# Input projection by seven block products for pairs of column tiles, in a phase ahead of attention, down and output projections

## The chip, the cores and the metric

The kernel runs on one core of one Trainium2 chip. The metric is device time in microseconds (us). Engines: PE (TensorE matmul; PEld is its weight load), DVE (VectorE), ACT (ScalarE), POOL (GpSimd), SP (SyncE, which issues the DMAs). Each has its own instruction queue and works through it in order; they meet at semaphores.

## The reference

One step of a one-layer encoder on 1024 prompt tokens and 32 sample tokens (1056 rows), width 1024, in fp32:

```python
h = _rmsnorm(x, g_mix)
z = h @ w_in                                   # 1056 x 1024 @ 1024 x 8192
qa, fa, va, ga, xb, gb, qc, gc, za, zb, zc = jnp.split(z, offs, axis=-1)
# A: HGRN2 recurrence, 4 heads x 128 (qa fa va ga, 512 columns each)
pa = (oa * silu(ga)) @ w_a_down                # 512 -> 1024
# B: causal conv + RG-LRU, width 1024 (xb, gb)
pb = (hb * silu(gb)) @ w_b_down                # 1024 -> 1024
# C: 4-head attention to 256 memory tokens (qc, gc, 512 columns each)
pc = (oc * silu(gc)) @ w_c_down                # 512 -> 1024
merged = sigmoid(za) * pa + sigmoid(zb) * pb + sigmoid(zc) * pc
y = x + merged @ w_out                         # then a final RMSNorm
```

Memory keys and values are projected from 256 memory rows; the states of conv, LRU and HGRN2 are outputs too.

## The kernel before

All activations lie transposed: 128 features on the partitions, tokens along the free axis, in three groups of 384, 384 and 288 (GN). Each large product is made of three fp32r matmuls: a value is split into a rounded part hi (ACT copy, L40) and a remainder lo (DVE subtract, L43), and mms (L46) issues hi*hi, hi*lo, lo*hi into one PSUM bank. The normalised h stays in SBUF as hh and hl for the whole kernel.

w_in is read in 64 tiles of 128 columns. A tile costs 8 (blocks of 128 rows) x 3 (products) matmuls in each token group: 24 with 384 columns, 24 with 384 and 24 with 288. wload (L107) loads a tile, wprep (L116) splits it, wtile (L132) issues its three groups through slot (L85). After each group, slot lets generator lists take a step: what the vector engines do with an earlier tile, and small matmuls, are so written into the queues between dense groups. PSUM: 3 dense banks (dbank, L68), 5 auxiliary (abank).

Order: phase 0 (norms of 2 memory and 9 token tiles: n_sq, n_mul, n_tr, n_out; projections of w_mem_k and w_mem_v, psmem). Then for B tiles 0 to 4 xb and gb (branch_b, L458: conv, gates pr/pi by matmul, sigmoid, tanh, exp, sqrt, scan), half of w_b_down, B tiles 5 to 7, then the gate logits za, zb, zc (psz) in turn with the down projections psdn (down, L575), with branch A (branch_a, L685; its chunk recurrence hgrn is advanced twice per token group) and branch C (branch_c, L879; chain and attn) ahead of their own down projections. state_out (L653) transposes the B states on PE (ptst), five steps after the last B tile. Everything that a branch makes stays in SBUF until its down projection reads it. At the end psout: merged by w_out for 9 token tiles, residual, final norm.

So every attention and recurrence step stands beside some input projection or down projection, and the DMAs are weights, inputs and outputs alone.

## Time and profile before

| | |
|---|---|
| median of 3 runs | 1197.78 us (1195.06 to 1199.65) |
| the profiled execution | 1196.16 us, span of its instructions 1194.4 us |
| mean granted TensorE clock | 0.997 |
| PE busy | 1179.8 us (99%), 7566 matmuls |
| DVE, ACT, POOL busy | 539.1, 479.9, 236.0 us (45%, 40%, 20%) |
| HBM | 63.49 MB read, 5.93 MB written |

A matmul's shown duration is its latency; matmuls overlap, so what one costs is the distance from one start to the next. The span is 1.8 us less than the execution's time.

### The profile page before, as it was taken

Reading aid. Unit: us, or ns where it says so; the run is one execution under the profiler, and the core shown is the slowest. Engines: PE = TensorE matmul, PEld = TensorE weight load, DVE = VectorE, ACT = ScalarE, POOL = GpSimd, SP = SyncE. Lnnn points to the kernel's source line nnn. Section 1 sums busy time; section 2 is a strip of 40 time slices with the busy share of each in tenths; the row PEclk is TensorE's granted clock in tenths of the full one; section 3 lists DMA queues with packets and bytes.
Section 4 is the critical chain, followed back from the end, with each engine's and each line's share of the span. In section 5 each row is a group of like instructions: output and inputs, shape, how many; then the busy total and the mean of one; then the engine's idle time right before and its main releaser. Section 6 shows DMA issues by size and latency. Waiting matters only on the chain.

```text
span 1194.4 us, 18697 instructions
## 1 busy us (share of the span) xinstructions
PE 1179.8 (99%) x7566; PEld 1161.6 (97%) x7566; DVE 539.1 (45%) x1052; ACT 479.9 (40%) x1043; POOL 236.0 (20%) x425
## 2 busy tenths in 40 slices
PE   8899999999999999999999999999999999999998
PEld 8899999999999999999999999999999999999996
DVE  5957775257711234454544411123456542236322
ACT  6567667367721114353434321111344452233211
POOL 4322222022202232121212101122000001223101
PEclk9999999999999999999999999999999999999999
DMA  8521101211111121111201111112111121105321
GB/s 274 169 63 39 40 21 45 80 38 39 37 36 53 44 63 38 36 43 35 57 27 55 38 32 35 52 44 58 44 46 44 41 54 44 54 27 176 106 93 40
DMA packets 113562, 70.63 MB, mean 59 GB/s; under 512 B 5560, under 2 KB 109668, under 8 KB 113476
## 3 DMA queue, kind: packets, MB, share of 16 engines
q1 hardware_dynamic: 113476, 69.44, 19.4%
q8 instruction: 59, 0.97, 0.4%
q14 instruction: 27, 0.22, 0.1%
HBM read 63.49 MB, written 5.93 MB: 58 GB/s over the span
## 4 chain that ended last, share of the span: by engine, by line
PE 92%; DVE 4%; DMA 2%; issue 1%; ACT 1%; SPq 0%; POOL 0%; POOLq 0%; DVEq 0%; ACTq 0%
PE psz L60 23%; PE psdn L60 14%; PE psgb L60 8%; PE psxb L60 7%; PE psout L60 7%; PE psfa L60 4%; PE psva L60 4%; PE psga L60 4%; PE psqa L60 4%; PE psqc L60 4%; PE psgc L60 3%; PE pr L60 1%; PE pi L60 1%; PE poc L60 1%; DVE ht L241 1%; PE pssa L60 1%
## 5 line engine op out<-in xcount | busy, mean ns | idle before, releaser
L43 DVE TENSOR_TENSOR wlo<-wraw,whi 128x1024 fp32r<-128x1024 f32 (+1 forms) x100 | 107.5, 1075 | 262.7 <-ACT whi L40 261.7
L60 PE MATMUL psz<-hh,whi 128*128 128x384 f32 (+1 forms) x576 | 185.9, 323 | 0.0
L60 PE MATMUL psz<-hh,wlo 128*128 128x384 f32 (+1 forms) x576 | 185.2, 321 | 0.0
L60 PE MATMUL psz<-hl,whi 128*128 128x384 f32 (+1 forms) x576 | 185.0, 321 | 0.0
L40 ACT ACTIVATE whi<-wraw 128x1024 fp32r<-128x1024 f32 (+1 forms) x104 | 96.3, 926 | 79.4 <-PE psdn L60 73.4
L60 PE MATMUL psdn<-ph,whi 128*128 128x384 f32 (+1 forms) x384 | 123.4, 321 | 0.0
L60 PE MATMUL psdn<-ph,wlo 128*128 128x384 f32 (+1 forms) x384 | 123.3, 321 | 0.0
L60 PE MATMUL psdn<-pl,whi 128*128 128x384 f32 (+1 forms) x384 | 123.2, 321 | 0.0
L60 PEld LDWEIGHTS psz<-hh,whi 128*128 128x128 f32 x576 | 108.1, 188 | 0.7 <-issue 0.6
L60 PEld LDWEIGHTS psz<-hh,wlo 128*128 128x128 f32 x576 | 108.2, 188 | 0.3 <-DVE wlo L43 0.3
L60 PEld LDWEIGHTS psz<-hl,whi 128*128 128x128 f32 x576 | 108.1, 188 | 0.0
L584 ACT ACTIVATE sz<-psz 128x384 f32<-128x384 f32 (+1 forms) x72 | 33.3, 463 | 181.7 <-PE psz L60 181.7
L60 PEld LDWEIGHTS psdn<-ph,whi 128*128 128x128 f32 x384 | 72.2, 188 | 0.0
L60 PEld LDWEIGHTS psdn<-pl,whi 128*128 128x128 f32 x384 | 72.1, 188 | 0.0
L60 PEld LDWEIGHTS psdn<-ph,wlo 128*128 128x128 f32 x384 | 72.1, 188 | 0.0
L60 PE MATMUL psout<-hl,mhi 128*128 128x384 f32 (+3 forms) x216 | 68.7, 318 | 0.5 <-DVE hl L43 0.5
L60 PE MATMUL psout<-hh,mlo 128*128 128x384 f32 (+3 forms) x216 | 68.6, 317 | 0.0
L60 PE MATMUL psout<-hh,mhi 128*128 128x384 f32 (+3 forms) x216 | 68.4, 317 | 0.0
L60 PE MATMUL psxb<-hh,wlo 128*128 128x384 f32 (+1 forms) x192 | 62.1, 324 | 0.0
L60 PE MATMUL psxb<-hh,whi 128*128 128x384 f32 (+1 forms) x192 | 61.9, 322 | 0.0
L60 PE MATMUL psxb<-hl,whi 128*128 128x384 f32 (+1 forms) x192 | 61.8, 322 | 0.0
L60 PE MATMUL psgb<-hh,wlo 128*128 128x384 f32 (+1 forms) x192 | 61.7, 321 | 0.0
(297 smaller groups left out, 2905.7 us busy)
## 6 DMA issues: line engine op xcount, KB each, us to landing
wraw<-in_w_in SPq DMA_DIRECT2D x64, 512.0 KB, 4.1
xt<-in_x_prompt SPq DMA_DIRECT2D x8, 512.0 KB, 5.1
wraw<-in_w_b_down SPq DMA_DIRECT2D x16, 256.0 KB, 2.8
wraw<-in_w_out SPq DMA_DIRECT2D x8, 512.0 KB, 4.4
xf<-in_x_prompt SPq DMA_DIRECT2D x8, 512.0 KB
out<-yf SPq DMA_DIRECT2D x8, 512.0 KB, 2.9
wraw<-in_w_mem_k SPq DMA_DIRECT2D x4, 512.0 KB, 3.7
wraw<-in_w_mem_v SPq DMA_DIRECT2D x4, 512.0 KB
```

The costliest lines, as they stand in the source:

```text
L40: nc.scalar.activation(out, in_, AF.Copy)
L43: (eng or nc.vector).tensor_tensor(out, a, hi.bitcast(F32), op=OP.subtract)
L60: nc.tensor.matmul(ps, a, b, start=st, stop=sp)
L241: nc.vector.scalar_tensor_tensor(hts[s][:n], xts[s][:n], rss[s][:n], gts[jobs[s][2]][:n], op0=OP.mult, op1=OP.mult)
L584: nc.scalar.activation(s, R["psz", g], AF.Sigmoid)
```

## The change

The 64 column tiles are taken in 32 pairs (c1, c2). The rows of w_in are halved (512 and 512), the features of h too, and the tokens are halved into two of 528 (HF). So one pair is a 2x2 block product, done by seven block products instead of eight (the Winograd form of Strassen's scheme): p1 = A11 B11, then with S1 to S4 made once from h, and T1, T2, a changed B12 and a changed B21 made per pair on POOL by four 128x512 subtractions. Each of the seven is a slot: 4 blocks x 3 products x 2 quarters of 264 tokens (QF) = 24 matmuls. X, Y, V, Z are PSUM tiles of two banks, two buffers in turn; the sums of products are formed partly in PSUM (slots 2, 5, 6 add to X, V, Z) and partly on DVE (post). Seven forms of h (A11, A12, A22, S1 to S4), each hi and lo, replace hh and hl; S1 to S4 and their splits are made between the norms and the first pairs.

All 32 pairs come first: eight B pairs in turn with z pairs, then per head two A pairs, a z pair and (one head later) a C pair. Their results go to DRAM scratch: sigmoids of z (zd), gc, qc, the B and A products (pbd, pad), memory keys and values. A second phase reads them back: down b with attention advanced beside it, down a, down c, out.

Core of the diff:

```diff
-T_BUFS, T2_BUFS = 45, 24
+T_BUFS, T2_BUFS = 36, 18
+W_RAW, W_HL, P_T, P_ZH = 9, 5, 8, 2
-    dense = ctx.enter_context(tc.tile_pool(name="dense", bufs=3, space=PS))
-    aux = ctx.enter_context(tc.tile_pool(name="aux", bufs=5, space=PS))
+    aux = ctx.enter_context(tc.tile_pool(name="aux", bufs=4, space=PS))
...
+        at(b - 8, loads)
+        at(b - 5, t1)
+        at(b - 4, t2)
+        at(b - 3, lambda: prep(0, "B11"))
+        at(b - 2, lambda: prep(1, "T2"))
+        at(b - 1, lambda: prep(2, "B21"))
+        at(b - 1, t3)
+        at(b, lambda: prep(3, "T1"))
+        at(b + 1, lambda: prep(4, "B12"))
+        at(b + 1, t4)
+        at(b + 2, lambda: prep(5, "B22"))
+        at(b + 3, lambda: prep(6, "B21"))
...
+    ACTS = ("A11", "S2", "A12", "S1", "S3", "S4", "A22")
...
+    def post(k, h):
+        v = lambda t: t[:, :, :QF]
+        if k == 0:
+            cur["p1"] = H("p1")
+            nc.scalar.activation(v2(cur["p1"]), v(cur["X"]), AF.Copy)
+        elif k == 1:
+            cur["u2"] = H("u2")
+            nc.vector.tensor_tensor(v2(cur["u2"]), v(cur["Y"]), v2(cur["p1"]), op=OP.add)
+        elif k == 2:
+            h.c11(v(cur["X"]))
+        elif k == 3:
+            cur["u4"] = H("p1")
+            nc.vector.tensor_tensor(v2(cur["u4"]), v(cur["V"]), v2(cur["u2"]), op=OP.add)
+        elif k == 4:
+            h.c22(v(cur["Z"]), cur["u4"])
+        elif k == 5:
+            h.c12(v(cur["V"]), cur["u2"])
+        else:
+            h.c21(v(cur["Z"]), cur["u2"])
...
+        name, new = (("X", 1), ("Y", 1), ("X", 0), ("V", 1), ("Z", 1), ("V", 0), ("Z", 0))[k]
...
+        for q in range(2):
+            qs = slice(q * QF, (q + 1) * QF)
+            o = ps[:, q, :QF]
+            for i in range(4):
...
+                nc.tensor.matmul(o, wh[:, i, :], fh[:, i, qs], start=st, stop=False, **kw)
+                nc.tensor.matmul(o, wh[:, i, :], fl[:, i, qs], start=False, stop=False, **kw)
+                nc.tensor.matmul(o, wl[:, i, :], fh[:, i, qs], start=False, stop=(i == 3), **kw)
+            advance(fast)
+            if q == 1:
+                advance(chains)
+                run_sched(s)
+        post(k, cur["h"])
...
+            tt(nc.vector, s1, a21, a22, OP.add)
+            tt(nc.vector, s2, s1, a11, OP.subtract)
+            tt(nc.gpsimd, a21, a11, a21, OP.subtract)
+            tt(nc.gpsimd, a12, a12, s2, OP.subtract)
...
+    for s in range(7 * NP):
+        if s == 7 * 16:
+            while chains:
+                advance(chains)
+            bstack.close()
+            a_setup()
+            chains.append(state_out())
+        slot(s)
...
+    slow.append(attention())
+    down("b", pB, 8, {2: lambda: zload("a", 0) if False else None, 6: lambda: late.append(prep_prods(pad, pA))})
+    zload("a", 0)
+    while late:
+        advance(late)
+    down("a", pA, 4, {})
+    while slow:
+        advance(slow)
+    zload("c", 0)
+    late.append(prep_prods(pcd, pC))
+    while late:
+        advance(late)
```

Three places in the queues. First, ACT where the chain of one B tile ends and that of the next begins: before, small steps by token group (whi splits a weight tile; xc and xbp read the conv input out of PSUM; r is the gate).

```order
L40 ACTIVATE whi<-wraw 128x1024
L467 ACTIVATE xc<-psxb,VT 128x384
L468 ACTIVATE xbp<-psxb 128x384
L541 ACT_TABLE_LOAD
L541 ACTIVATE r<-r,sneg 128x384 x2
L541 ACTIVATE r<-r,sneg 128x288
```

And ACT in the change, from the square root of one tile (th) over the first steps of the next (xw, sgb) to the reading of X after slot 0 of the z pair (p, the tile p1 of the code).

```order
L669 ACT_TABLE_LOAD
L669 ACTIVATE th<-th 128x1056
L42 ACTIVATE whi<-wraw 128x512 x2
L42 ACTIVATE whi<-T_1658 128x512
L42 ACTIVATE whi<-wraw 128x512
L626 ACTIVATE xw<-xbp,VT 128x1059
L627 ACT_TABLE_LOAD
L627 ACTIVATE sgb<-gb 128x1056
L42 ACTIVATE whi<-T_1620 128x512
L270 ACTIVATE p_1804<-X 128x528
```

The chain's steps are now whole rows of 1056, and the reading of X stands behind three of them and a table load in ACT's queue.

Second, PE at the attention of the last head: before, its last products (poc) stand between dense groups of psz.

```order
L60 MATMUL psz<-hh_83,wlo 128x384
L60 MATMUL poc<-prh,mh 128x256
L60 MATMUL poc<-prl,mh 128x256
L60 MATMUL poc<-prh,ml 128x256
...
L978 MATMUL poc<-prs,cv 128x32 x2
L60 MATMUL psz<-hh_84,whi 128x384
```

In the change, from the last matmul of down a on (scores pssa and pssb, transposes ptp of the exponentials ex).

```order
L62 MATMUL psdn<-ph,wlo 128x288
L1098 MATMUL ptc<-ident,ck 128x128 x2
L62 MATMUL pssa<-mh,qh 128x256
...
L62 MATMUL pssb<-mh,ql 128x256
L1146 MATMUL ptp<-ident,ex 128x128 x6
L62 MATMUL pssa<-mh,qh 128x256
```

From there all three groups' scores, transposes and products of head 3 follow each other with no psdn between them; the next psdn row is that of down c.

Third, SP where the phases meet, in the change alone (before, only weight and input loads stand here): the last stores of the first phase, then the first loads of the second (sz are sigmoids of z, praw the B products).

```order
L155 DMA gcd_115<-zh 128x528
L155 DMA qcd_119<-zh 128x528 x2
L155 DMA gcd_115<-zh 128x528
L956 DMA wraw<-in_w_b_down 128x8x128
L1001 DMA sz<-zdb_96 128x384 x2
L1001 DMA sz<-zdb_96 128x288
L975 DMA praw<-pbd_120 128x384 x2
L975 DMA praw<-pbd_120 128x288
L956 DMA wraw<-in_w_b_down 128x8x128
```

Every load of the second phase now stands behind the store of the last pair's last quarter.

## Rows read from the trace of the kernel before

**Rows 1.** The page, parts 1 and 4: busy engines; chain that ended last, by engine.

```profile
PE 1179.8 (99%) x7566; PEld 1161.6 (97%) x7566; DVE 539.1 (45%) x1052; ACT 479.9 (40%) x1043; POOL 236.0 (20%) x425
PE 92%; DVE 4%; DMA 2%; issue 1%; ACT 1%; SPq 0%; POOL 0%; POOLq 0%; DVEq 0%; ACTq 0%
```

**Rows 2.** The chain in order of time, merged: start us, us, what.

```profile
76.05 3.19 PE psgb L60 x24
355.10 5.76 PE psdn L60 x36
360.86 11.53 PE psz L60 x72
```

**Rows 3.** Timeline, PE and DVE, end of phase 0: start us, us, what, [idle before].

```profile
43.77 0.28 PE L60 MATMUL psmem<-hh,whi 128*128 128x256 f32 x1
...
45.44 0.28 PE L60 MATMUL psmem<-hh,wlo 128*128 128x256 f32 x1
49.87 0.43 PE L60 MATMUL psxb<-hh,whi 128*128 128x384 f32 x1
55.62 1.09 PE L251 MATMUL pt<-ident,ht 128*128 128x128 f32 x8 [1.33 <-DVE ht L241]
61.81 0.54 DVE L43 TENSOR_TENSOR hl<-pt,hh 128x128 fp32r<-128x128 f32 x2 [1.97 <-ACT hh L40]
```

**Rows 4.** Timeline of POOL and DVE, phase 0: a subtraction on POOL, two norm multiplies.

```profile
28.14 2.41 POOL L43 TENSOR_TENSOR wlo<-wraw,whi 128x1024 fp32r<-128x1024 f32 x1 [0.57 <-ACT whi L40]
28.64 3.00 DVE L241 SCALAR_TENSOR_TENSOR ht<-xt,rsr,gx 128x1024 f32<-128x1024 f32 x1
34.75 1.28 DVE L241 SCALAR_TENSOR_TENSOR ht<-xt,rsr,gx 128x1024 f32<-128x1024 f32 x1
```

**Rows 5.** Groups by line and form, DVE and ACT: xcount | busy us, mean ns | idle.

```profile
L43 DVE TENSOR_TENSOR wlo<-wraw,whi 128x512 fp32r<-128x512 f32 x32 | 22.7, 708 | 73.5 <-ACT whi L40 72.6
L552 DVE TENSOR_TENSOR_SCAN xc<-r,ig 128x384 f32<-128x384 f32 x8 | 7.7, 958 | 0.3
L40 ACT ACTIVATE whi<-wraw 128x1024 fp32r<-128x1024 f32 x72 | 76.2, 1058 | 25.6 <-PE psdn L60 19.7 <-PE psmem L60 4.4 <-DMA wraw<-in_w_mem_k 1.5
L40 ACT ACTIVATE whi<-wraw 128x512 fp32r<-128x512 f32 x32 | 20.1, 628 | 53.8 <-PE psdn L60 53.8
L506 ACT ACT_TABLE_LOAD x8 | 10.3, 1283 | 0.1
L501 ACT ACTIVATE th<-r,spos 128x384 f32<-128x384 f32 x16 | 10.1, 631 | 0.0
```

**Rows 6.** Timeline, one step of the recurrence in branch A.

```profile
502.20 0.39 PE L803 MATMUL pu<-v,kt 128*128 128x128 f32 x2
503.57 0.26 ACT L796 ACTIVATE kt<-pu 128x128 f32<-128x128 f32 x1
```

**Rows 7.** Timeline, one token group of attention, head 0: scores, scaling, split of transposes.

```profile
840.15 0.28 PE L60 MATMUL pssa<-mh,qh 128*128 128x256 f32 x1
844.67 0.35 DVE L955 TENSOR_SCALAR ex<-ex,ri 128x256 f32<-128x256 f32 x1
849.55 0.82 PE L963 MATMUL ptp<-ident,ex 128*128 128x128 f32 x6
850.67 1.02 DVE L43 TENSOR_TENSOR prl<-ptp,prh 128x384 fp32r<-128x384 f32 x2 [3.56 <-ACT prh L40]
```

**Rows 8.** Windows (busy us of each engine, clock, DMA share, GB/s), and DMA issues.

```profile
20.00:30.00 10.00, 9.94 (x87) 9.74 (x85) 7.46 (x9) 8.09 (x16) 7.41 (x6) 1.00 0.92 292
...
wraw<-in_w_b_down SPq DMA_DIRECT2D x16, 256.0 KB, 2.8
```

**Rows 9.** Windows near the start: PE, PEld, DVE, ACT, POOL busy; PEclk.

```profile
8.00:9.00 1.00, 0.00 (x0) 0.00 (x0) 1.00 (x1) 0.00 (x0) 0.03 (x1) 1.00 1.20 367
...
11.00:12.00 1.00, 1.00 (x7) 1.00 (x6) 0.84 (x2) 1.00 (x2) 0.00 (x0) 0.50 1.06 267
...
13.00:14.00 1.00, 1.00 (x10) 1.00 (x10) 0.70 (x1) 0.40 (x1) 0.00 (x0) 0.93 1.12 406
```

More of the change, by code (lines that the diff above doesn't have):

```diff
@@ L377, in feed @@
             yield
-            for s in range(4, 10):
+            for s in range(4, nj + 2):
                 norm_step(s)
+                if s == 8:
+                    forms.append(form_ops())
                 yield
-        start(feed())
+            done[0] = True
+        chains.append(feed())
         for n in range(8):
@@ new lines @@
+            if n == 3:
+                chains.append(vec_consts())
+            chains.append(mem_evac(which, j, ps))
+            advance(chains)
+            advance(forms)
+        while not done[0]:
+            advance(chains)
+            advance(forms)
+        while chains:
+            advance(chains)
+        run_sched(-3)
+        while forms:
+            advance(forms)
+        run_sched(-2)
+        run_sched(-1)
+    fb = p1stack.enter_context(tc.tile_pool(name="forms_b", bufs=1, reuse_waits="tile"))
@@ L653, in state_out @@
     def state_out():
-        for _ in range(5):
-            yield
         pt = abank("ptst")
@@ L865, in branch_a @@
[L865 to L872 removed]
+            nc.vector.tensor_scalar(f[:, :NT], f[:, :NT], oml[:, j:j + 1], lb[:, j:j + 1], op0=OP.mult, op1=OP.add)
+            yield
+            lf, b = T1("lf"), T1("b")
+            nc.scalar.activation(lf[:, :NT], f[:, :NT], AF.Ln)
@@ new lines, in KS, with slot2 @@
+    def KS(name):
+        return (kp.tile([128, NT], F32R, tag="kh", name=name + "h"), kp.tile([128, NT], F32R, tag="kl", name=name + "l"))
+    slow, late = [], []
+    par = [0]
+    def slot2(ms, after=None):
+        issue(ms)
+        par[0] = (par[0] + 1) % 2 if len(ms) == 12 else 0
+        if par[0] == 0:
+            advance(slow)
+        if after is not None:
+            after()
+        advance(late)
+    loaded, prepped, wtiles = {}, {}, []
+    for src, kt in (("w_b_down", 8), ("w_a_down", 4), ("w_c_down", 4)):
+        for it in range(8):
+            wtiles.append((I[src][0], kt, it * 128))
@@ new lines, in branch_c, with attention @@
+        ev_qc(0)
+        yield
+        kvsplit(1, vr)
+        ev_qc(1)
+        for t in range(8):
+            if t in (2, 4, 6):
+                trans(t // 2 - 1)
+            if t in (3, 5, 7):
+                pv(t // 2 - 1)
+            if t in (0, 2, 4):
+                scores(t // 2)
+                scale_(t // 2)
+            if t == 1:
+                ev_qc(2)
+            if t < 7:
+                yield
+    def attention():
+        for j in range(4):
+            yield from branch_c(j)
@@ L1028, in xload, with wgen @@
             nc.sync.dma_start(xf[t][:n], xs[t])
-    down(lambda k: prods_c[k], C_ZC, "last", AH_C, lambda: next_phase("fp", 1))
+    def wgen():
+        for k in range(6):
+            wout_load(k)
+            yield
+            yield
+            wout_prep(k)
+    down("c", pC, 4, {1: lambda: late.append(wgen())})
+    while late:
+        advance(late)
+    for k in range(6, 8):
+        wout_load(k)
+        wout_prep(k)
     gf = wpool.tile([128, D], F32, tag="hi", name="gf")
@@ L1079, in after @@
                 xload(t + 3)
-        slot(ms, after)
+        slot2(ms, after)
         advance(late)
@@ L1089 @@
             out_unit(t, gi)
-    assert not fast and not slow and not tail and not late
-    phase.close()
+    assert not fast and not slow and not late and not chains
 _INS = ['x_prompt', 'x_sample', 'mem_prompt', 'cache_mem_k', 'cache_mem_v', 'state_hgrn', 'state_conv', 'state_lru',
```

1366 lines of the change are left out of this document (706 added, 660 removed).

## Prediction

> **What bounds the kernel now.** I read the page's shares first: PE is busy for 1179.8 us of a span of 1194.4, the other engines for less than half, and the chain that ended last is 92% PE [rows 1]. So the time is PE's own work, and the chain in order of time shows at what pace: 24 matmuls of 288 columns take 3.19 us (132.9 ns each), a column tile of w_in 11.53 us (so 173.8 ns for each of its 48 of 384), a down tile of four blocks 5.76 us, each starting where the last ended [rows 2]. Then the timeline for the one place that is not so dense, the end of phase 0: the first projection matmul starts at 49.87, a wait of 1.33 us for a norm follows, and the last norm tile is written at 62.35 [rows 3]. Whatever shortens PE's work shortens the kernel, as long as PE still has something to do at each moment; that second condition is what the change touches.
>
> **The saving.** 15 matmuls of 256 columns start from 43.77 to 45.44, 119.3 ns apart [rows 3]; between that and 132.9 for 288, a matmul of 264 columns takes 119.3 + (8/32) x 13.6 = 122.7 ns, a slot of 24 takes S = 2.94 us. Before: 64 tiles x 11.53 = 737.9 us. After: 32 pairs x 7 slots x 24 = 5376 matmuls x 122.7 = 659.6. **-78 us**. It is not the eighth of 738 (92), because a matmul costs about 13 ns beyond its columns at 2.4 GHz and there are 768 more. Gates, recurrence, attention, down and out keep their matmuls (the gates' quarters of 264 cost 0.05 us more per tile).
>
> **Phase 0.** Before, the first projection group runs while late norms are made; counting its wait and the transposes in between (3.6 us), projection starts in effect at 53.5. After, S1 to S4 need every token. Up to the last norm the work of PE, DVE and DMA is much the same, so it ends at about 59 (62.35 less the 4 us that it stood behind a projection group). Then, from 0: DVE makes s1 and s2, four half operations of 1056 columns at 1.3 us (1.28 for 1024 [rows 4]); POOL a21 and a12, four at 2.5 us (2.41 for 1024); then DVE owes five forms of two 1.3 us remainders and four weight remainders of 0.7 us [rows 5]: 5.2 + 13 + 2.8 = 21 us on DVE, 10 on POOL. PE can run slots 0 and 1, but slot 2 waits for p1, which stands on ACT behind all five form copies; the fourth of them waits for POOL, so p1 is ready at about 22, and slot 3 waits for u2, behind all remainders on DVE, at about 25. Contiguous work would have been at 8.8 there: 16 us idle at least. One row shows more: beside a POOL subtraction from 28.14 to 30.55 a DVE multiply that takes 1.28 us alone took 3.00 and ended 1.1 us after POOL did [rows 4]. So POOL's work adds to DVE's in part; if all of it did, u2 would be ready at about 32 and PE idle for 23. I take 19, with 5.5 for the later start: **+24** (10 if ACT and DVE interleave well and the norms end sooner, 32 if all adds).
>
> The Trainium skill states this as a rule (SBUF — State Buffer, section Who interferes with whom): DVE operations with two SBUF inputs and POOL operations that read SBUF take an exclusive lock, the loser waits for the whole instruction. The row above agrees. By the rule alone phase 0 would be +29 instead of +24.
>
> **The B pairs.** Each reading of a PSUM tile has one slot of slack before PE needs the tile again: p1 (ACT) before slot 2, u2 before 3, c11 before 4, u4 before 5, c22 before 6, c12 and c21 (DVE) before the next slots 0 and 1. These readings stand in their queues behind the chain of the last B tile, now in whole rows of 1056: on DVE 1.3 us each and 2.8 for the scans (0.958 for 384 [rows 5]), on ACT 1.1 to 1.2 (1.058 for 1024, 0.628 for 512, more with an operand per partition) and 1.28 per table load. Followed from slot 2 of a B pair (time 0; ACT comes to exp 0.5 before it): exp with its table load ends at 2.0, POOL's square at 4.5, DVE's th at 6.6 (one POOL subtraction in its way), sqrt 7.7, weight copy 8.3, remainder 9.0, u4 9.7; slot 5 wanted it at 3S = 8.8: **0.9 late**. Then DVE: ig, remainder, c22, scans, remainder, c12, 6.9 us to 16.6; the next slot 0 wanted it at 5S + 0.9 = 15.6: **1.0 late**. Then the last multiply, remainder and c21 to 19.6, and on ACT xw, table load, sigmoid, copy, p1 to 24.4; slot 2 of the z pair wanted it at 7S + 1.9 = 22.5: **1.9 late**. The rest of the z pair is light and the delay does not build up. 3.8 x 7 tiles (the eighth is the next part): **+28**. Bounds: 8 if only one of the waits binds; 50 if DVE becomes the limit: per two pairs DVE has 14 remainders, 10 readings and 13.6 us of chain, 31 us, POOL 16, together 47 where PE has 44.
>
> **state_out.** Ahead of slot 112 the rest of the eighth chain is written at once, and ptst follows slot 112 on PE; it needs POOL's copy of the scan's end. From the last gate matmul: four sigmoids 2.0, tanh 1.2, table and exp 2.5, square 2.5, th 1.3, sqrt 1.1, ig 1.3, scans 2.8, copies 0.8 = 15.7 us, of which slot 112 covers 2.9. Behind ptst stands all of PE. **+13** (8 to 18). Before, the same transpose was written five steps later, between psz groups.
>
> **A pairs.** The recurrence's kt comes 1.63 us after its pu started [rows 6], the next is due after 12 matmuls (1.47) and a step of about 1 us. Slack 0.85; ACT's copy and reading (1.25 per slot) and DVE's come between, and three times per head PE waits for pot with 4 banks instead of 5. About 2.5 per head: **+10** (3 to 25).
>
> **Where the phases meet.** All loads stand behind the last store on SP, so nothing is fetched until 1.3 us after the last slot. Ahead of the eighth B product lie two weight tiles, two rows of sz, eight of praw, six of attention: 7.8 MB. At 292 GB/s, the best ten-microsecond window, that is 27 us; at 275, 28; a 256 KB load lands 2.8 us after its issue, 1.9 of it not transfer [rows 8]. PE ends the first down tile at about 34, with 11.5 us of work in it: **+23** (14 to 30).
>
> **Down a to down c.** Attention needs 49 steps, down b and a give 37; head 3 from its scores on is left to the drain. One token group takes 4.9 us from its first score matmul to its scaled exponentials, and 2.1 more from transposes to their remainders [rows 7]. With about 3 us of DVE work first, three groups in a row take 24 us, 8 of them PE's own. Then the store of the last product, and loads of sz and four products (2.7 MB, 9.8 us at 275 GB/s, with landing and splits some 15) which all stand behind it; the first tile has 5.8 us of work, so 9 us more of idle. **+25** (15 to 35).
>
> **The rest.** Two of eight w_out tiles are prepared after down c: **+2** (0 to 4). In the trace PE did nothing from 8 to 9; from 11 to 12 the granted clock was 0.50, the level of 1.2 GHz, and late in 13 to 14 it was back at 2.4 [rows 9]. That is some 4 us at half rate, 2 us lost; three long idles at that price: **+6** (0 to 15).
>
> **Sum.** -78 + 24 + 28 + 13 + 10 + 23 + 25 + 2 + 6 = +53. On the profiled execution's 1196.2 us, which lies within the three runs and 1.6 under their median: **1249 us**.
>
> **Rivals.** (1) *DVE and ACT keep up.* They are below half busy now, and each reading has a slot of slack. Then phase 0 falls to 10, the B pairs to 8 at most, A to 3, the clock to 0: 24 + 28 + 10 + 6 becomes 21, about 1202; with the B pairs at 0 and the meeting at its lower end, 1185, faster. It decides where all costs together come under 78; the four gaps that depend on no queue (phase 0, state_out, meeting, drain) are 85 by themselves. Chance 0.17, of it 0.12 faster. (2) *DVE is the limit in the B half.* POOL's and DVE's work add up (47 us for 44): 50 instead of 28, and phase 0 at 32: about 1280. For it the row of 3.00 us [rows 4], against it the light z pairs. 0.20. It is what the lock of the Trainium skill's page SBUF — State Buffer (Who interferes with whom) would do here. (3) *The seven products don't save what they should*, the matmul of 264 columns costing as much as that of 288, 132.9 ns: 714 us, saving 24, about 1303. Against it the 119.3 of 256 columns. 0.04. My forecast, 1215 to 1270: 0.55; the rest lies between.
>
> **Numbers.** 0.5% is 6 us, about what a measurement can tell from no change. Faster 0.13, same 0.06, slower 0.81. The range of 1195 to 1285 leaves about 0.15 below and 0.05 above.
>
> **What would show it.** After: X, Y, V, Z matmuls 122 to 123 ns apart inside a slot; PE busy well under 95%; PE waits by tile: S forms and p1 before the first V, then V for DVE, X for ACT once per B pair, ptst for POOL by about 13 us, psdn of the first tile for praw, pssa/ptp/poc after down a for DVE and ACT. I am wrong if the slots of the B pairs follow each other without waits, if the loads at the meeting are spread over the first phase's end, or if head 3's drain takes under 10 us.

## The result, and the profile after

The changed kernel takes 1292.62 us (median of 4 runs, 1290.78 to 1296.88) where the kernel before takes 1197.38 (4 runs beside it): a ratio of 1.080, 95% interval 1.076 to 1.084. It is slower, by 95 us; 53 were forecast, and the time lies 8 us above the range. The profiled execution is 1294.4 us with a span of 1292.4.

The page first: part 1, and of part 2 the granted clock in 40 equal slices.

```profile
PE 1149.5 (89%) x8382; PEld 1114.1 (86%) x8382; DVE 762.4 (59%) x1152; ACT 529.4 (41%) x1026; POOL 403.0 (31%) x463
PEclk9868999999999997999999999999899999699999
```

PE is busy for 30 us less than in [rows 1], and idle for 143 us where it was idle for 15. The granted clock is below nine tenths in some of the slices. The stretches show where. Columns as in [rows 8]: the stretch, its length, busy time of PE, PE's weight loads, DVE, ACT and POOL, granted clock, DMA share, GB/s.

```profile
0.00:68.36 68.36, 49.78 (x354) 47.12 (x354) 43.70 (x77) 36.18 (x69) 26.25 (x38) 0.89 0.64 195
68.36:98.44 30.08, 9.30 (x50) 8.79 (x49) 26.33 (x21) 12.58 (x15) 24.27 (x7) 0.61 0.18 53
98.44:488.17 389.73, 359.67 (x2833) 353.53 (x2833) 278.57 (x298) 196.00 (x301) 147.75 (x131) 0.98 0.25 76
488.17:898.26 410.09, 384.29 (x3079) 374.94 (x3077) 221.61 (x354) 167.38 (x356) 132.87 (x168) 0.98 0.22 68
898.26:925.88 27.62, 13.38 (x56) 11.70 (x55) 12.73 (x26) 12.18 (x28) 0.00 (x0) 0.75 0.96 305
925.88:1090.70 164.82, 161.72 (x1016) 157.50 (x1014) 90.56 (x217) 49.06 (x124) 29.27 (x50) 0.99 0.40 123
1090.70:1127.74 37.04, 17.84 (x71) 13.14 (x69) 17.01 (x49) 11.72 (x34) 3.75 (x11) 0.64 0.30 94
1127.74:1183.00 55.26, 51.20 (x289) 49.64 (x289) 42.16 (x69) 24.69 (x46) 25.04 (x23) 0.93 0.65 210
```

They are: phase 0 up to the first slot; the first two slots and the wait for the forms; slots 2 to 111 (the B half); slots 112 to 223 (the A half); the meeting; down b and a; the drain; down c. A busy PE can be PE at half clock, so I set each stretch against what its matmuls need at full clock: 121.3 ns for 264 columns (row below), 173 for 384 [rows 2], 132.9 for 288, 119.3 for 256, 108 to 112 for 128. For the B half that is 110 slots of 2.91 and 192 gate matmuls, 343.5 us of 389.7.

| stretch | length | needed | lost | forecast |
|---|---|---|---|---|
| phase 0, to slot 2 | 98.4 | 45.8 | 52.6 (before, up to 60: 13.4) | +24 |
| B half | 389.7 | 343.5 | 46 | +28 |
| A half with ptst | 410.1 | 369.8 | 40 | +23 |
| meeting | 27.6 | 8.6 | 19 | +23 |
| down b and a | 164.8 | 153.7 | 11 | 0 |
| drain | 37.0 | 8.4 | 29 | +25 |
| down c and out | 164.6 | 146.2 | 18 | +2 |

The same count gives 36 us lost in the kernel before (13 of them before 60 us, 7 in the attention stage, 7 after it), so 180 more are lost and PE's work is 82 less: the 98 us between the two spans. The seven products themselves came as forecast. Two matmuls of a slot, first and last of 24 (start, us, engine, line, operation):

```profile
143.07 0.28 PE L302 MATMUL Y<-S2h,whi 128*128 128x264 f32 x1
...
145.86 0.28 PE L304 MATMUL Y<-S2h,wlo 128*128 128x264 f32 x1
```

23 steps in 2.79 us: 121.3 ns, a slot of 2.91 us. 224 slots take 652 us, against 737.9 before: 86 saved, 78 forecast.

What PE waited for, whole span (who <- for whom: us in total, times, longest). In the trace's names p is p1 (line 270) or u4 (line 278), u is u2.

```profile
PE X L302 <- ACT p L270: 23.0, 8, 15.3
PE psdn L62 <- ACT ph L42: 20.4, 4, 8.2
PE V L302 <- DVE p L278: 12.4, 8, 1.8
PE pt L362 <- DVE ht L352: 12.4, 7, 4.1
PE ptst L685 <- POOL ST L678: 12.0, 1, 12.0
PE V L302 <- DVE u L273: 10.4, 12, 1.5
PE ptc L1098 <- DMA ck<-in_cache_mem_k: 9.0, 3, 6.0
PE pot L876 <- DVE on L869: 7.9, 4, 2.0
PE ptp L1146 <- DVE ex L1138: 6.3, 7, 3.4
PE X L304 <- DVE wlo L45: 5.5, 1, 5.5
```

The forecast named most of these. New are the wait of slot 0 for a weight remainder (5.5) and the cached keys (9.0).

### The profile page after: what moved, and what is told of

Its sections match the earlier page's. It is cut to its first block, busy times and chain, and to the rows that moved or that the text cites. A ratio compares the mean times of both kernels' runs of the same rounds, so it can differ in the third digit from the quotient of the medians.

```text
span 1292.4 us, 21318 instructions
## 1 busy us (share of the span) xinstructions
PE 1149.5 (89%) x8382; PEld 1114.1 (86%) x8382; DVE 762.4 (59%) x1152; ACT 529.4 (41%) x1026; POOL 403.0 (31%) x463
## 4 chain that ended last, share of the span: by engine, by line
PE 54%; DVE 17%; ACT 10%; DMA 8%; issue 7%; POOL 3%; SPq 1%; DVEq 0%; POOLq 0%; ACTq 0%
PE psdn L62 10%; PE psout L62 7%; DVE wlo L45 5%; PE V L302 4%; PE V L304 3%; PE V L303 3%; PE Z L302 3%; PE Z L304 3%; PE Z L303 3%; ACT whi L42 2%; PE X L302 2%; PE X L304 2%; PE X L303 2%; POOL hT L498 2%; DMA wraw<-in_w_in 2%
## 5 line engine op out<-in xcount | busy, mean ns | idle before, releaser
L45 DVE TENSOR_TENSOR wlo<-wraw,whi 128x512 fp32r<-128x512 f32 (+1 forms) x193 | 193.5, 1004 | 113.9 <-ACT whi L42 113.8
L42 ACT ACTIVATE whi<-wraw 128x512 fp32r<-128x512 f32 (+1 forms) x200 | 123.9, 639 | 59.2 <-PE Z L303 17.7
L302 PE MATMUL X<-A12h,whi 128*128 128x264 f32 x256 | 75.7, 296 | 23.0 <-ACT p L270 23.0
L302 PE MATMUL V<-S4h,whi 128*128 128x264 f32 x256 | 76.2, 298 | 12.4 <-DVE p L278 12.4
L302 PE MATMUL V<-S1h,whi 128*128 128x264 f32 x256 | 76.4, 298 | 10.4 <-DVE u L273 10.4
L1011 POOL TENSOR_TENSOR sz<-sz 128x384 f32<-128x384 f32 (+1 forms) x48 | 50.9, 1080 | 80.6 <-DVE sz L1010 80.4
L302 PE MATMUL Y<-S2h,whi 128*128 128x264 f32 x256 | 75.0, 293 | 0.4
L302 PE MATMUL X<-A11h,whi 128*128 128x264 f32 x256 | 75.0, 293 | 0.0
L304 PE MATMUL V<-S4h,wlo 128*128 128x264 f32 x256 | 74.9, 292 | 0.0
L303 PE MATMUL V<-S4l,whi 128*128 128x264 f32 x256 | 74.5, 291 | 0.0
L303 PE MATMUL V<-S1l,whi 128*128 128x264 f32 x256 | 74.3, 290 | 0.0
```

Source lines behind the costliest of these rows:

```text
L42: nc.scalar.activation(out, in_, AF.Copy)
L45: (eng or nc.vector).tensor_tensor(out, a, hi.bitcast(F32), op=OP.subtract)
L302: nc.tensor.matmul(o, wh[:, i, :], fh[:, i, qs], start=st, stop=False, **kw)
L303: nc.tensor.matmul(o, wh[:, i, :], fl[:, i, qs], start=False, stop=False, **kw)
L304: nc.tensor.matmul(o, wl[:, i, :], fh[:, i, qs], start=False, stop=(i == 3), **kw)
L1011: nc.gpsimd.tensor_tensor(m, m, z, op=OP.add)
```

## The experiments

My theory after the result: the seven products save what they should; the waits are links of in-order queues (one late operation on ACT or POOL delays a reading that stands behind it), not full engines. The rivals: DVE is the limit wherever PE waits; or the division into two phases costs it all, whatever the products. Ratios are to runs of the kernel before made beside each version, gains in us to the 1292.6 of the changed kernel. Its four runs spread over 6 us (1290.8 to 1296.9): the gains of 5 to 6 us below are just clear of that spread, one of 3 isn't.

**e1: ptst later.**

```
-            chains.append(state_out())
+            chains.append(state_late())   # 14 yields, then state_out
```

> The changed kernel with the transposition of the B states (ptst) written 14 slots later, nothing else. In the changed kernel PE waited 12.0 us for it, and the granted clock was 0.5 for about 14 us around it. If the place of that one instruction is the cause, the 12 us disappear, the clock stays full there, and the time falls by 12 to 18 us, from 1292.6 to 1275 to 1281. The rival: PE waits for the drained eighth chain in any case, at another instruction (the gates or the next reading of a bank); then the wait turns up under another name and the time falls by less than 4 us.

1282.9 us, ratio 1.072 [1.070, 1.074]: 10 less. The wait for ST is gone; in its place PE waits 4.8 us for p1 in slot 114, because ACT still has the drained eighth chain to do first. Partly the rival, then.

**e2: the differences on DVE.**

```
-            tt(nc.gpsimd, a21, a11, a21, OP.subtract)
-            tt(nc.gpsimd, a12, a12, s2, OP.subtract)
+            tt(nc.vector, a21, a11, a21, OP.subtract)
+            tt(nc.vector, a12, a12, s2, OP.subtract)
```

> The changed kernel with the two differences A11-A21 and A12-S2 made on DVE instead of POOL. On POOL they took 21.4 us (four of 5.35) while DVE's remainders beside them were stretched from 1.2 to 2.9 each. If the two engines take turns (the lock), DVE alone needs 69.28 to about 93 for the forms instead of 97.7, PE's slot 2 starts 4 to 6 us earlier, and the time falls by 4 to 6 us, to about 1287. If instead POOL and DVE work side by side and POOL is only slow, 4.8 us more on DVE make it later: the last remainder ends at about 100 and the time rises by 2 us or so.

1287.5, ratio 1.076 [1.074, 1.078]: 5 less, as the lock says. The rows of the changed kernel (POOL, then DVE; x2 are two operations):

```profile
70.59 14.62 POOL L498 TENSOR_TENSOR hT<-hT 128x1056 f32<-128x1056 f32 x2 [13.36 <-DVE s L498]
85.17 6.81 POOL L498 TENSOR_TENSOR hT<-hT,s 128x1056 f32<-128x1056 f32 x2
83.98 5.72 DVE L45 TENSOR_TENSOR S3l<-hT,S3h 128x1056 fp32r<-128x1056 f32 x2 [3.48 <-ACT S3h L42]
89.74 5.60 DVE L45 TENSOR_TENSOR S4l<-hT,S4h 128x1056 fp32r<-128x1056 f32 x2
```

and of e2, all on DVE:

```profile
74.67 2.41 DVE L498 TENSOR_TENSOR hT<-hT 128x1056 f32<-128x1056 f32 x2
85.83 2.41 DVE L45 TENSOR_TENSOR S3l<-hT,S3h 128x1056 fp32r<-128x1056 f32 x2
```

Two operations take 2.41 us on DVE alone; beside POOL the same remainders took 5.72. While DVE had an unbroken row of them (69.28 to 80.4), POOL's first two took 14.62. This agrees with the exclusive lock that the Trainium skill states (SBUF — State Buffer, Who interferes with whom). POOL's first operation was done at about 82.9, where ACT's copy of its result began: 12 us for one operation, behind a whole row of DVE's and not behind a single one.

**e3: own buffers for raw w_out tiles.**

```
-            wraws[k] = wpool.tile([128, D], F32, tag="raw", name="wraw2")
+            wraws[k] = wop.tile([128, D], F32, tag="wo", name="wraw2")   # bufs=2, loaded two ahead
```

> The changed kernel with two buffers of their own for the raw w_out tiles, which are loaded two ahead, instead of the pair that they share with the w_c_down tiles. In the changed kernel the down projection of c took 61 us from its first to its last matmul for 46 us of matmuls, with loads of 3.3 us, a copy and a remainder one after the other on the chain. If the shared buffers are the cause, that stage falls by 8 to 12 us and the time to about 1282. If the cause is DVE (77% busy in that stage, POOL's additions in its way), it falls by less than 4.

1286.5, ratio 1.076 [1.073, 1.078]: 6 less. Down c takes 49.5 us instead of 55.3 (not the 61 of the text), at a DVE of 94%. In the changed kernel each w_out load had stood behind the release of a w_c_down tile. The gain lies between the figures of the two theories: the shared buffers cost some of the stage, and with them gone DVE is close to full.

**e4: order of loads.**

```
     wload(0)
+    raws = [load_prod(src) for src in pbd]
     zload("b", 0)
```

> The changed kernel with the loads at the meeting of the phases in another order: the first weight tile, the eight products, then the gate row, the next weight tile and the loads of attention. In the changed kernel 27 us pass from the last slot to the dense part of the second phase, at 313 GB/s and a DMA share of 0.99. If bandwidth sets it, 0.5 + 4.3 MB ahead of the last product instead of 8.4 MB let PE reach its eighth product at about 16 to 18 us instead of 25: the time falls by 6 to 9 us, to about 1285. If latency or the splitting of products (eight of about 2 us on ACT and DVE, 16 us in all) sets it, it falls by less than 4.

1293.7, ratio 1.081 [1.079, 1.084]: nothing gained. The rows of ACT tell why:

```profile
903.74 5.38 ACT L42 ACTIVATE ph<-praw 128x384 fp32r<-128x384 f32 x12
921.57 0.52 ACT L1092 ACTIVATE tg<-graw 128x384 f32<-128x384 f32 x1 [12.46 <-DMA graw<-gcd]
922.00 2.41 ACT L42 ACTIVATE ph<-praw 128x384 fp32r<-128x384 f32 x6
```

Four products were split by 909; then attention's tanh, whose load now came last, held the queue for 12.5 us with four products behind it. A load moved back is a wait moved forward on the engine that reads it in program order.

**e5: p1 and u2 ahead of the last forms.**

```
     S2, S1 split
+    slot(0)
+    slot(1)
     S3, S4, A22 split
```

> The changed kernel with the first pair's slots 0 and 1 and their readings p1 and u2 written ahead of the copies and remainders of S3, S4 and A22, and with buffers for p1 and u2 that don't lie where hT lay. In the changed kernel p1 stood on ACT behind all five form copies, was made at 97.8, and slots 2 and 3 (whose forms A12 and S1 were ready at 80.5) came after that. If the order on ACT and DVE is the cause, slots 2 and 3 run before 97 and the time falls by 5 to 7 us, to about 1286. If the forms as such set the end of phase 0 (slot 4 needs S3, and the reading of X a buffer that hT held), slot 4 starts where slot 2 started and that is the whole gain, 5.8; a gain under 3 would mean that DVE's extra reading delays the remainders as much as it helps.

1289.5, ratio 1.078 [1.076, 1.079]: 3 less, not clear of noise. The trace shows what moved. Slot 2 now follows slot 1 at 82.8, but slot 3 waits 8.3 us for u2: u2 stands on DVE behind a weight remainder, that on ACT's copy, that on POOL's weight subtraction, and this on POOL behind the two differences, until 91.6. One link of the chain removed, the next one held.

**e6: attention after every group of down a.**

```
-        par[0] = (par[0] + 1) % 2 if len(ms) == 12 else 0
+        par[0] = 0
```

> The changed kernel with one step of attention after every group of the down projection of a instead of after every second one, so that 48 of its 49 steps are written beside down groups and head 3 is not left to a drain. In the changed kernel 38 us pass between the last matmul of down a and the first of down c, of which PE's own work is 9.4 at full clock. If uncovered attention is the cause, what is left is the store of the last product, the loads and the splits, 12 to 15 us, and the time falls by 15 to 23 us, to about 1273. The rival: a step of attention takes longer on DVE and ACT than a group of 12 matmuls of PE (2.1 us), so the same waits move into down a, and the time falls by less than 8.

1278.4, ratio 1.067 [1.065, 1.069]: 14 less. Head 3's scores and products now lie between the groups of down a with waits of 0.5 us in all; left are 4.4 and 2.6 for cached keys and 6.6 for the last product.

**e7: a third pair of banks.**

```
+    banks(n_aux=2, n_dense=3)            # B half; 4 and 2 elsewhere
+        pr, pi = pg[:, :n], pg[:, 256:256 + n]   # both gates in one bank, pieces of 256
```

> The changed kernel with three pairs of PSUM banks for X, Y, V and Z in the B half instead of two (and two single banks for the gates instead of four, with both gates of 256 columns in one bank and a fifth piece of 32 columns). Each reading then has a second slot of slack. In the changed kernel PE waited some 29 us in the B half for p1, u2 and u4, 4.7 us in each of the tiles. If late readings on in-order queues with one slot of slack are the cause and no engine is full, at least two thirds go, and the time falls by 18 to 28 us, to about 1270. If DVE is the limit (POOL's and DVE's work taking turns, 47 us for 44 of PE), the waits stay and only change their names: less than 8.

1291.7, ratio 1.079 [1.076, 1.082]: no gain. Waits of PE in the B half, in the changed kernel (105 to 487 us):

```profile
PE V L302 <- DVE p L278: 12.4, 8, 1.8
PE V L302 <- DVE u L273: 9.5, 8, 1.5
PE X L302 <- ACT p L270: 7.7, 7, 1.5
```

and in e7:

```profile
PE X L310 <- ACT p L278: 12.5, 7, 1.8
PE Z L310 <- DVE gb L618: 10.2, 7, 1.5
PE V L310 <- DVE p L286: 5.0, 7, 0.7
```

29.6 us there, 27.7 here. Waits that stay and change their names are what the text gave for a full DVE, so this run by itself doesn't rule that out; e9 does. The lines have another reason as well: p1, u4 and c22 read a tile that PE goes on adding to two slots later, in the same bank, so a third pair of banks gives these three readings no slack.

**e8: PE kept busy in three waits.** 40 transpositions of the identity ahead of slot 0, 60 ahead of slot 2, 60 ahead of down b.

> The changed kernel with idle transpositions of the identity on PE where it waits anyway: 40 ahead of the first slot, 60 ahead of the first pair's slot 2, 60 ahead of the second phase. They give PE work of about 6.5 us each at full clock and delay nothing that is ready. In the changed kernel the granted clock was 0.5 for 17 us from 63.5, for 17 us from 87.4, and for two stretches of 6.8 from 903 and 917. If the clock falls because PE stands idle, these stretches shrink, slot 2 takes 2.9 us instead of 5.2, and the time falls by 4 to 8 us, to about 1287. If the clock there doesn't matter, because something else sets the pace, nothing changes (within 2 us).

1287.2, ratio 1.076 [1.074, 1.077]: 5 less. Granted clock from 60 to 80 us 0.91 instead of 0.59, from 80 to 104 0.79 instead of 0.64, from 900 to 930 0.89 instead of 0.77.

**e9: two ACT operations of the B chain one slot later.**

```
-        nc.scalar.activation(sg[:, :NT], G[:, :NT], AF.Sigmoid)
         (copies of the states)
         yield
+        nc.scalar.activation(sg[:, :NT], G[:, :NT], AF.Sigmoid)
...
         th = (xc + 1) * th                                     # DVE
+        yield
         nc.scalar.activation(th[:, :NT], th[:, :NT], AF.Sqrt)
```

and one yield less between the last gates' sigmoids and the tanh.

> The changed kernel with two of the B chain's ACT operations written one slot later (the sigmoid of G after xw, the square root after the multiply that it reads), and two light steps made one, so that the chain still has 14. In the changed kernel's B pair the square root waited on ACT for DVE's th; behind it stood a weight copy, behind that on DVE a remainder and u4, which PE's slot 5 waited 1.75 us for; and the sigmoid with its table load stood ahead of p1, which the z pair's slot 2 waited for, and then u2. If such chains of waits across the in-order queues are the cause, the 12.4 us for u4 and most of the 17 for p1 and u2 go, and the time falls by 15 to 25 us, to about 1273. If DVE's own load is (73% busy, with POOL's subtractions stretching its operations), the waits move to c12, c22 or another reading and the time falls by less than 6.

1267.2, ratio 1.058 [1.057, 1.060]: 25 less, the largest single gain. The chain of waits as the changed kernel has it (ACT, then DVE; slot 5 had been due at 154.7):

```profile
152.89 1.09 ACT L669 ACTIVATE th<-th 128x1056 f32<-128x1056 f32 x1 [1.88 <-DVE th L668]
153.89 1.14 ACT L42 ACTIVATE whi<-wraw 128x512 fp32r<-128x512 f32 x2
154.53 1.43 DVE L45 TENSOR_TENSOR wlo<-wraw,whi 128x512 fp32r<-128x512 f32 x1 [1.68 <-ACT whi L42]
155.89 0.69 DVE L278 TENSOR_TENSOR p<-V,u 128x528 f32<-128x528 f32 x1
```

and the B half of e9 (105 to 455 us):

```profile
PE V L302 <- DVE u L273: 11.5, 14, 1.4
PE V L302 <- DVE p L278: 1.2, 1, 1.2
```

DVE and POOL have the same operations as before; only the order changed. So a full DVE isn't what bounded the B half: slots 2 to 111 take 26 us less with the same work. 17 of the 26 are the waits (29.6 to 12.7). The three stretches at half clock inside the B half are gone too, which is 5 us. The moves of e9 were not run one by one.

**e10: eight ordinary products in the same two phases.** No forms of sums, no subtractions of weights, four weight blocks split instead of seven.

```
-    ACTS = ("A11", "S2", "A12", "S1", "S3", "S4", "A22")
+    ACTS = ("A11", "A12", "A11", "A12", "A21", "A22", "A21", "A22")
```

> The two phases of the changed kernel with eight ordinary products of 24 matmuls per pair instead of the seven (A11 B11 + A12 B21 and so on: no forms of sums, no subtractions of weights, four weight blocks split instead of seven, every result read once). PE gets 32 x 24 matmuls of 121 ns more, 93 us. If about half of what the seven products save on PE goes into their own waits (19 to 22 us at the forms, some 25 at the readings in the B half), it takes only 30 to 45 us more than the seven: 1322 to 1338. If all of the loss lies in the division into two phases (the meeting, the drain, the stores and loads), which both have, it takes 85 to 93 us more: 1378 to 1386.

1298.9, ratio 1.085 [1.083, 1.087]: only 6 more than the seven, below both theories' figures. From slot 4 to ptst no wait of PE is listed:

```profile
66.17:93.09 26.92, 26.08 (x193) 25.77 (x193) 11.41 (x18) 10.12 (x13) 1.29 (x2) 0.88 0.38 100
93.09:480.00 386.91, 376.21 (x3098) 376.01 (x3096) 173.57 (x192) 165.58 (x243) 56.76 (x68) 0.99 0.24 72
```

(The last ten of these 387 us are the wait for the drained eighth chain, at ptst.) Of the 93 us that seven products take off PE, 87 went back into what only the seven lose: by the count of the table 23 us ahead of slot 2, 46 in the B half (the eight lose 0.5 there) and 19 in the A half. The eight stand 102 us above the kernel before, with 7 of it in projection matmuls (745 us for 738). The other 95 lie in what both versions share: the two phases with their stores and loads, the chain in whole rows, the order of the steps, the smaller buffers. No run here takes these apart, and none has the seven products without the phases; e18 takes 42 of them back by order and buffers alone.

**e11: e4's order, attention held until the last block of the first down tile, and e6.**

```
-                    if k % 2:
+                    if k == kt - 1 or c != "b" and k % 2:
                         advance(slow)
```

> The changed kernel with the order of loads of the run e4 (products first), attention's first steps held until the last block of the first down tile, and attention advanced after every group as in the run e6. In e4 the gain was lost because attention's tanh, which waits for its loads, stood on ACT ahead of the copies of products 4 to 7 (ACT idle from 909 to 921.6). If bandwidth and this one place set the meeting, the first down tile ends some 8 us earlier than in e6: 1278.4 - 8 = about 1270. If latency or splits set it, it stays at e6's 1278, or rises by what three lost steps of attention cost at the end of down a (up to 8 us).

1281.3, ratio 1.070 [1.068, 1.072], 3 above e6, whose runs overlap with its own. At the meeting it is ahead: 34 us after its last slot it has begun 118 down matmuls, the changed kernel 91. The end of down a takes it back: between down a and down c 20.0 us pass without a down matmul, in e6 9.7, and the three lost steps of attention fall there.

**e12: sums of the first half of the columns before the last norms.**

```
+                if s == 10:
+                    done[1] = True     # columns 0:264 of s1, s2, a21, a12 may be made, on DVE
```

> The changed kernel with the sums S1, S2, A11-A21 and A12-S2 made for the first half of the token columns while the norms of the last tokens still run, all on DVE. In the run with all differences on DVE the forms ended about 5 us earlier than in the changed kernel. Half of the 9.6 us of sums now lies beside the norms, where DVE was some 70% busy. If DVE's work after the last norm sets the end of phase 0, PE's slot 2 starts 4 to 5 us earlier still than in that run, and the time falls to about 1283 (10 under the changed kernel). If the norms are already bound by DVE (PE waited 12.4 us for their multiplies), what is gained behind the last norm is lost ahead of it: about 1287.

1287.4, ratio 1.075 [1.072, 1.077], as e2 within the interval. The agreement with the second figure of the text is luck, for the edit moved nothing. The first of the sums stands behind the last norm copy (71.74 to 72.0), as in e2, where it starts at 70.00:

```profile
72.27 1.24 DVE L497 TENSOR_TENSOR s<-hT 128x1056 f32<-128x1056 f32 x1
```

So this is e2 once more, with the forms' operations in another order, and its question stays open. Slot 0 started at 71.4 (69.1 in e2), but all of that delay was there before any sum: the third norm multiply from the end started at 54.41, in e2 at 52.09.

**e13 and e14: together.** e13 has the edits of e1, e2, e3, e5, e6, e8 and e9; e14 those and the five named in its text.

> The single changes of the runs before in one kernel: the B chain's two ACT operations one slot later, ptst 14 slots later, the differences on DVE, p1 and u2 ahead of the last forms, own buffers for raw w_out tiles, attention after every group of down a, transpositions that keep PE busy in three waits. Their gains by themselves against 1292.6: 25.4, 9.7, 5.1, 3.1, 6.1, 14.2, 5.4, together 69. If they are independent: about 1224. If waits hide behind each other (the ACT queue at ptst and in the B chain, DVE at the end of phase 0), a fifth to a third of it is lost: 1238 to 1248.

> The kernel of the run e13 with five more edits: the forms' first half of columns early; the last head's product split straight from SBUF instead of stored and loaded, and the other three products and the first gate row of c fetched during the last tile of down a (PE waited 6.3 us there for a product); the order of loads of e4 with attention held until the last block of the first down tile, and four extra steps of attention in down b; four buffers instead of two for keys and cached keys (PE waited 9.0 us for cached keys). If each goes for what its wait says (5, 7, 5, 8) this takes another 20 to 25 us: about 1200, as the kernel before. If the waits are taken over by the next one in line (attention's own chain of scores, scaling, transposes), about 1212.

e13: 1234.9, ratio 1.032 [1.030, 1.033], 58 of the 69 us: the causes add up but for a sixth. e14: 1241.3, ratio 1.037 [1.035, 1.039], slower than e13. In both of them stands this (e13, PE; line 289 are the idle transpositions):

```profile
86.48 6.71 PE L289 MATMUL warm<-ident 128*128 128x128 f32 x60
92.95 0.37 PE L309 MATMUL X<-A12h,whi 128*128 128x264 f32 x1
```

With e2 and e5 nothing waits there any more, and the filler itself is the wait. Of what e14 loses against e13, 4 us are there when slot 2 starts (97.0 against 93.0) and 3 come behind the last slot, where PE waited 11.2 us for cached keys instead of 6.5: more buffers for loads that are still issued late don't help. The early sums of e12 are late in e14 too.

**e15 to e17: which of the remaining waits.** e15 is e13 without those 60 transpositions, with these two edits and four buffers instead of two for the keys; e16 and e17 add to e15.

```
+            if t == 3 and j < 3:
+                fetched[j + 1] = fetch(j + 1)            # e15: the next head's loads
+            split(own[0][0][:, cs], own[0][1][:, cs], s)  # e15: head 3, in place of store and load
+                if c == "b" and g == 1 and it % 2 == 0:
+                    advance(slow)                         # e16, with e11's order
+                if k == 0:
+                    post(k, cur["h"])                     # e17: p1 ahead of the chain's step
```

> The kernel of the run e13 without the 60 idle transpositions ahead of slot 2 (there they stood in the way: slot 1 ended at 86.4, they at 92.9, and slot 2 followed at once), with each attention head's loads issued five steps before the head begins, and with the last head's product split straight from SBUF while the first three products of c are fetched during the last tile of down a. If the waits in the trace of e13 are what they seem (6 us at slot 2, 6.5 for cached keys, 6.5 for the last product), it takes 1234.9 - 14 to 19: 1216 to 1221. If attention's own chain takes over at the drain, 1225 or more.

> The kernel of the run e15 with the load order of e4, attention's steps held until the last block of the first down tile, and four extra steps of attention in down b instead. With the loads of heads now ahead of their use, the four extra steps make good the three that are held, so that the gain of the order shows: 4 to 6 us under e15. If the meeting is bound by splits and latency, or the extra steps bring new waits in down b, within 2 us of e15 or above it.

> The kernel of the run e15 with p1 written ahead of the chain's step in slot 0, the sigmoid of G one more slot later, and in the A half the transposes of the normed rows one step later (with a second buffer for them, paid with one raw weight buffer). In e13 PE waited 11.8 us for u2, 5.9 for the normed rows. If these readings stand behind the chains' operations on ACT and DVE as u4 did, 10 to 15 us go: about 10 to 15 under e15. If the eighth raw buffer that is left makes weight loads late, a new wait for weights takes some of it; if the chain's steps only move (the scan later, u4 late again), less than 4.

e15: 1221.3, ratio 1.021 [1.019, 1.022]. e16: 1216.8, ratio 1.017 [1.015, 1.019]. Both as their waits said; the cached keys are gone from PE's list. e17: 1248.9, ratio 1.044 [1.042, 1.046], 28 slower than e15. Its waits:

```profile
PE V L309 <- ACT xbp L627: 13.8, 7, 2.0
PE V L309 <- DVE u L273: 9.9, 11, 1.2
PE V L309 <- DVE p L278: 8.8, 12, 4.1
```

On ACT, p1 now waits 2.3 us for X with the gates' sigmoids, tanh, table load and exp behind it, and the second reading of X (xbp) behind those. The normed rows' wait (5.9 in e15) is gone, but po and pu wait 6.6 us longer. The run has four edits at once (three orders and one raw buffer less), and none was run alone, so which of them costs what is read from these rows and not shown.

**e18: the eight products with the same mending.** The edits of e1, e3, e6, e15 and e16 on e10. It lacks e2, e5 and e9, which mend what the eight don't have, and the fillers of e8.

> The eight products of the run e10 with those edits of e16 that have nothing to do with the seven: ptst later, attention after every group and its loads ahead, the last product from SBUF, load order, w_out's own buffers. Its trace has 11.2 us at ptst, 8.3 at cached keys, 23 lost at the drain, 8 in down c, 9 at the meeting; mending them as in e14 to e16 gives 36 to 44 us: 1255 to 1263. Then the mended seven (1216.8) keep about 40 us of the 93 where the seven as they were kept 6. If it comes under 1235, the eight gain as much by the same mending as the seven did, and the seven's own waits are as they were; if it comes to 1280 or more, it has waits that the seven hid.

1256.9, ratio 1.050 [1.048, 1.052], as expected. The mended seven (1216.8) keep 40 of their 93 us, the seven as they were kept 6; some of the 40 may be e8's fillers, worth 5 by themselves. No version here is faster than the kernel before.

## Why the prediction was right in kind and too small

**The saving** was right: 121.3 ns for 264 columns (122.7 taken), 86 us (78). The rival by which such a matmul costs as one of 288 is out.

**Phase 0** failed in its first step: "Up to the last norm the work of PE, DVE and DMA is much the same, so it ends at about 59". The last norm copy ended at 69.0. The delay against the kernel before comes between two of DVE's norm multiplies: the fourth from the end starts at 42.06 (before, 40.22), the third at 52.91, and the last two are still as far behind as that one. The rows of that stretch (SP, ACT and DVE of the changed kernel, then DVE before):

```profile
36.97 3.02 SPq L135 DMA_DIRECT2D wraw<-in_w_in  x4
40.04 0.50 SPq L135 DMA_DIRECT2D wraw<-in_w_mem_v  x1
...
46.31 0.63 ACT L42 ACTIVATE whi<-wraw 128x512 fp32r<-128x512 f32 x1 [4.90 <-DMA wraw<-in_w_mem_v]
48.12 0.42 DVE L445 COPY om<-ptm 128x256 f32<-128x256 f32 x1 [4.18 <-DMA out<-om]
52.91 2.30 DVE L352 SCALAR_TENSOR_TENSOR ht<-xt,rsr,gx 128x1024 f32<-128x1024 f32 x1
...
44.38 1.28 DVE L241 SCALAR_TENSOR_TENSOR ht<-xt,rsr,gx 128x1024 f32<-128x1024 f32 x1
```

ACT waited 4.9 us for a half block of w_mem_v, whose load is issued behind four loads of the first w_in blocks; the next norm's square and the first split of A11 stood behind that on ACT. DVE stood still for 4.2 us in the same time, until a store of memory keys or values (om) issued behind the same loads had landed, then for 1.5 until ACT had copied A11, and only behind A11's remainder came the multiply. PE waited 12.4 us in all for these multiplies (6.0 before). So the sentence was wrong in two ways: the loads come in another order, and the splits of A11 and A12 now stand between the norms. Every trace here of a version in two phases has this wait of ACT (3.7 to 4.9 us), the kernel before has none there; no run moved the loads, so the cause is read from the rows and not shown. From there on the working held: u2 was ready at 100.6, 31.6 us behind the last norm, near the 32 that I gave "if all of it did" add, and PE was idle for 20.8 (19 taken). Two slots before slot 2's start is 92.6, against 53.5: +39 for 24. Of the 15 more, 10 are the later norms, 2 the idle, and some 3 the half clock at which slots 0 and 1 ran (9.3 us of PE's time for 5.8 us of work).

**The B pairs** were right in their waits, 29.6 us for 28, and not in all their places: u4 was 1.75 late (0.9 forecast), p1 0.5 to 1.5 (1.9), u2 0.6 to 1.5 (none forecast), c12 never (1.0). That the total agrees is in part luck. The chain that I followed had the square root behind th, but not what stands behind the square root. e9 settles the cause; e7 shows that a third pair of banks doesn't mend it. The other 17 us lost there are the clock (6 us at half rate from 98.4 and three stretches of 3.4, 8 lost) and short pauses. Rival 1, by which DVE and ACT keep up, is out with these waits. Rival 2, DVE as the limit, is out as well: in e9 DVE does the same work and slots 2 to 111 take 363.7 us instead of 389.7.

**state_out** 12.0 for 13, **the meeting** 19 for 23, **the drain** 29 for 25: right, in place and size. e1 takes most of the first back, e6 and e15 most of the third. Of the second e16 takes 4.5. The meeting isn't bandwidth alone: order helped there only with attention's reading held back as well (e4 against e11 and e16). **A pairs**: waits of 13.1 for 10.

**The rest** failed: "Two of eight w_out tiles are prepared after down c" was so, but it was the other six that cost. Their loads shared two buffers with the w_c_down tiles. Down c and out lost 18 us (7 before), for 2 forecast; e3 gives 6 of them back.

**The clock** is by this count the term that was furthest off in size: "three long idles at that price: +6". In the trace there are 18 stretches at a granted clock of 0.5, the level of 1.2 GHz: in phase 0, at ptst, the meeting and the drain, and single ones in the halves and in down a and c. PE was busy for 78 us in them, where full clock would have needed 39 (before, 3.4 us of work in one stretch). Of the 39 some 10 fall in phase 0 and 13 at the meeting and the drain, partly beside waits, and 13 in the two halves. What the 39 cost in time is shown for a part alone: e8 fills three waits and gets 5 us back; in e16, where PE waits less, 34 us of work are at that level.

The losses were forecast at 131 us and came to 180: 15 more in phase 0, 18 in the B half, 17 in the A half (8 of these two the kernel before lost in the same work), 9 in down c and out, 4 in down b and a, and the 6 that stood for the clock are in these rows. Three sums of the forecast don't come out, and none of them decides: 3.8 x 7 is 26.6 and not 28, the steps of state_out add up to 15.5 and not 15.7, and the upper end of phase 0, with 23 us of idle and the 5.5 of the later start, is 29 and not 32. What the short pauses in the halves are, some 8 us each beside waits and clock, I have not settled.

## What to carry to other kernels

Fewer matmuls buy time only if the readings between them keep pace: here seven products instead of eight took 93 us off PE and gave 6, and at most 40 once the waits were mended. Look at what stands in front of each reading on its in-order engine, across engines and not by load alone: an operation that waits there for another engine should be written a step after the one it waits for, which was worth 25 us for two moved lines. It is no rule to apply blindly: e17 moved more such lines and lost 28. And price the granted clock at every place where PE pauses, not at the long idles alone.

## What I had not expected of the hardware

POOL's two subtractions beside an unbroken row of two-input DVE operations took 14.62 us for the pair, where one of about the same size had taken 2.41 [rows 4]; and a 128x512 weight remainder on DVE rose from 708 ns [rows 5] to 995 on average. POOL's weight subtractions are only a part of that: in e10, which has none, it is 817.

The granted clock fell inside the B half, where PE stood still for less than 2 us at a time, and not at each of the like waits: up to 156.6 and up to 206.4 PE waited the same 1.75 us for u4, the clock stayed full behind the first and was 0.5 behind the second:

```profile
204.00:206.00 2.00, 0.69 (x6) 0.47 (x4) 1.67 (x2) 1.57 (x4) 1.22 (x1) 1.00 0.00 0
206.00:210.00 4.00, 3.56 (x17) 3.56 (x18) 4.00 (x5) 0.41 (x1) 0.00 (x0) 0.60 0.00 0
210.00:214.00 4.00, 4.00 (x34) 4.00 (x33) 4.00 (x5) 0.00 (x0) 2.11 (x3) 0.97 0.01 4
```

PE did 17 matmuls in four microseconds and 34 in the next four.
